# Two sets of four PSUM banks for W_down's seven Strassen products, and halo rows with high and low weight parts on their own column groups

## The chip, the cores and the metric

The kernel runs on one core of one Trainium2 chip. The metric is the device time of one execution in microseconds (us), as the median of several runs of the same program. A core has five engines with instruction queues of their own: PE (TensorE, matrix products into the eight banks of PSUM), DVE (VectorE), ACT (ScalarE), POOL (GpSimd) and SP (SyncE, which here issues the DMAs). They wait for each other through semaphores.

## The reference, cut to what matters

One decoder layer over 1024 tokens and 16 meta tokens, in float32:

```
h  = concat(meta, x)                                   # (1040, 1024)
xn = rms_norm(h, mix_pre_g)
mix = [ rms_norm(SSD(xn)), rms_norm(stick_breaking_attention(xn)) ] @ w_out
h  = h + rms_norm(mix, mix_post_g)
xn = rms_norm(h, ffn_pre_g)
gu = xn @ w_up                                         # (., 2 * 2816)
g  = causal_dwconv3(gu[:, :2816])                      # 3 taps, looks 2 tokens back
f  = (gelu(g) * gu[:, 2816:]) @ w_down                 # (., 1024)
h  = h + rms_norm(f, ffn_post_g)
return h[16:]
```

Because the convolution looks two tokens back, the last two meta tokens (the halo rows) go through the output projection and the first norms too.

## The kernel before, in words

**Arithmetic.** A float32 product is made of three products: each operand is split into a high part (a copy to the float32r type by ACT) and a low part (the operand less its high part), and high x high, low x high and high x low are summed in PSUM.

**Stages.** Norm and projections, SSD, attention (with W_out's first half as filler work on PE), W_out's second half with the norms behind it, W_up by a seven-product Strassen scheme, then W_down, from 1531 us to the end. In the attention stage (L971 on) only PE's order is written out by hand, and the other engines' order is made by the framework's planner. From the sixth row block of W_out's second half to the end (L1400 to L1788) the orders of PE, DVE, ACT and POOL are as the code writes them.

**W_down (L1549 to L1788).** The tokens are two halves of four row blocks t = 0 to 3, the 2816 rows of w_down 11 pairs p, the 1024 output columns two halves. `DOWN` (L38) lists seven products in the order 1, 2, 3, 6, 5, 7, 4; each is 11 steps, one for each pair, 77 steps s in all (`steps2`, L1551). `down_mm` (L1643) issues a step: for each of the four row blocks (order 3, 0, 1, 2) three matmuls of 128x512. Each product sums in four banks of its own. When a product is done, `evac2` (L1654) carries the banks into four groups of SBUF sums `facc[h, hf, t]` (h: half of the tokens, hf: half of the columns): by ACT copies for products 1 and 3, by DVE adds for the rest, two for each row block after products 5 and 7; after product 6 another four DVE adds join sums in SBUF (L1768). These jobs go to a list, `todo`, of which one is taken in each loop step.

The loop (L1718) does in step s: `down_mm(s)`; loads; `split_step(s + 3)` (L1568), in which ACT makes the high parts and DVE the low parts of the two operands of step s + 3, in a ring of three buffers, so that it waits for step s to end; for product 6 DVE first makes the operand t2 = b22 - b11 (L1579). Then come sums of w_down's blocks by `W_SUMS` (L1588: b11 in steps 15 + 2k, b21 in 16 + 2k and 41 + k, b12 in 37 + k, for k = 0 to 10), and one job of `todo`. In the last 14 steps (`LATE`, L1552) POOL instead of DVE makes the low part of the weight operand (L1582). The very last step has buffers of its own, and is split ahead of its turn (L1754 to L1758).

A finished row block gets its tail: `half_tail` (L1682: ACT sums the squares, DVE multiplies by the gain), `scale_tail`, `close_tail` (L1695: POOL adds the two halves and takes the power -0.5) and `end_tail` (L1700: DVE scales and adds the residual, SP stores). The tails of the first half of the tokens run from `todo` during product 7. The last four steps run row block by row block (L1722 to L1733), each block followed by `evac2` for product 4 and its tail.

**Halo rows.** `halo_rows` (L901) multiplies the two rows with W_out's halves: once in the attention stage (L1014), once before W_out's second half (L1067). Each of the four 32-column groups of PE holds a quarter of the output columns (256), and sums 8 blocks x (high, low). ACT copies the four quarters out of PSUM (L910) and SP stores them (L911) to `halod[half]`. `halo_block` (L1167) reads both, scales each by its own factor (L1173, L1175) and runs the norms of `after` (L1095).

Of the kernel before, what the change touches and what calls it, by code (L numbers as in the profile page):

```python
# [16 lines left out]
P = 128  # L17
# [34 lines left out]
def tile_layer(ctx: ExitStack, tc: tile.TileContext, x, meta, rows, parts,  # L52
# [16 lines left out]
    def psum_mm(name):  # L69
        return ps.tile([P, 512], F32, tag="mm", name=name, bufs=2)  # L70
# [62 lines left out]
    halod = [dr.tile([2, D], F32, name=f"halod{n}", tag=f"halod{n}") for n in range(2)]  # L133
# [767 lines left out]
    def halo_rows(pool, half, y0, w, acc):  # L901
        for k in range(8):
            for s in range(2):
                for c in range(4):
                    mm(acc[32 * c:32 * c + 2, 0:256], y0[:, k, :], w[k][s][:, 256 * c:256 * c + 256].bitcast(F32),
                       start=k == 0 and s == 0, stop=k == 7 and s == 1)
        mh = pool.tile([P, 256], F32, tag="ma", name=f"mh{half}", bufs=1)
        for c in range(4):
            rows_ = slice(32 * c, 32 * c + 2)
            nc.scalar.activation(mh[rows_], acc[rows_, 0:256], AF.Copy)  # L910
            nc.sync.dma_start(out=halod[half][:, 256 * c:256 * c + 256], in_=mh[rows_])  # L911
# [255 lines left out]
    def halo_block():  # L1167
        mt, mo = wp_f32("whi", "mb0")[:2], wp_f32("wlo", "mo0")[:2]
        for n, r in enumerate((r_ssd, r_sb)):
            dst = mt if n == 0 else mo  # L1170
            nc.sync.dma_start(out=dst, in_=halod[n])
            if n == 0:
                nc.vector.tensor_scalar(mt, mt, r[:2, 0:1], None, op0=ALU.mult)  # L1173
            else:
                nc.vector.scalar_tensor_tensor(mt, mo, r[:2, 0:1], mt, op0=ALU.mult, op1=ALU.add)  # L1175
# [376 lines left out]
    n2, LATE = len(steps2), 14  # L1552
# [15 lines left out]
    def split_step(s):  # L1568
        n, a, b, p = steps2[s]
        if s < n2 - 1:  # L1570
            hi = wp.tile([P, 2, 512], F32R, tag="whi", name=f"dh{s}", bufs=WB)
            lo = wp.tile([P, 2, 512], F32R, tag="wlo", name=f"dl{s}", bufs=WB)
            hi, lo = ([t[:, k] for k in range(2)] for t in (hi, lo))
        else:
            hi, lo = ([da.tile([P, 512], F32R, tag=f"b11{2 * k + e}", name=f"d{e}{k}{s}") for k in range(2)] for e in range(2))
        sub = nc.vector.tensor_tensor
        if n == 6:
            wd["t2", p] = db.tile([P, 512], F32, tag="t2", name=f"t2_{p}", bufs=2)
            sub(wd["t2", p], wd["b22", p], wd["b11", p], op=ALU.subtract)  # L1579
        for k, raw in enumerate((araw.pop(s), wd[b, p])):  # L1580
            nc.scalar.activation(hi[k], raw, AF.Copy)  # L1581
            (nc.gpsimd.tensor_tensor if k and s >= n2 - LATE else sub)(lo[k], raw, hi[k].bitcast(F32), op=ALU.subtract)  # L1582
        dops[s] = hi, lo
# [59 lines left out]
    def down_mm(s, tbs):  # L1643
        n, a, b, p = steps2[s]
        hi, lo = dops[s]
        for t in tbs:
            if p == 0:
                banks[t] = psum_mm(f"dn{n}_{t}") if t == 3 else pse.tile([P, 512], F32, tag="dn", name=f"dn{n}_{t}",
                                                                        bufs=6)
            c = slice(t * P, (t + 1) * P)  # L1650
            for i, (u, v) in enumerate(((hi, hi), (lo, hi), (hi, lo))):
                mm(banks[t], u[0][:, c], v[1], start=(p == 0 and i == 0), stop=(p == NPR - 1 and i == 2))  # L1652

    def evac2(n, t, acc):  # L1654
        add = nc.vector.tensor_tensor
        if n == 1:
            nc.scalar.activation(facc[1, 0, t], acc, AF.Copy)
        elif n == 2:
            add(facc[0, 0, t], acc, facc[1, 0, t], op=ALU.add)
        elif n == 3:  # L1660
            nc.scalar.activation(facc[0, 1, t], acc, AF.Copy)
        elif n == 6 or n == 4:
            add(facc[1, 0, t], acc, facc[1, 0, t], op=ALU.add)
        elif n == 5:
            add(facc[0, 1, t], acc, facc[0, 1, t], op=ALU.add)
            add(facc[1, 1, t], acc, facc[1, 0, t], op=ALU.add)
        elif n == 7:
            add(facc[1, 0, t], acc, facc[1, 0, t], op=ALU.add)
            add(facc[1, 1, t], acc, facc[1, 1, t], op=ALU.add)
# [12 lines left out]
    def half_tail(h, t, hf):  # L1682
        fg, ht, ms = tails[h, t]
        f = facc[h, hf, t]
        c = slice(512 * hf, 512 * hf + 512)
        junk = db.tile([P, 512], F32, tag="t2", name=f"jt{h}{t}{hf}", bufs=2)
        nc.scalar.activation(junk, f, AF.Square, scale=D ** -0.5, accum_out=ms[:, hf:hf + 1])
        nc.vector.tensor_tensor(fg[:, c], f, gfp[:, c], op=ALU.mult)
# [22 lines left out]
    last_u = probs[-1]  # L1711
    todo = []
# [5 lines left out]
    for s in range(n2):  # L1718
        n, a, b, p = steps2[s]
        if s > 2 and s < n2 - 4:  # L1720
            down_mm(s, (3, 0, 1, 2))
        elif s == n2 - 4:  # L1722
            for act in todo:
                act()
            for t in range(4):
                for k in range(4):
                    down_mm(s + k, (t,))
                evac2(n, t, banks[t])
# [8 lines left out]
        elif s == 5:  # L1737
# [4 lines left out]
            for h in range(2):  # L1742
                for hf in range(2):
                    for t in range(4):
                        facc[h, hf, t] = db.tile([P, 512], F32, tag=f"fa{h}{hf}{t}", name=f"facc{h}{hf}{t}")
# [6 lines left out]
        if s + 5 < n2:  # L1752
# [10 lines left out]
        if p == NPR - 1:  # L1763
            for t in (3, 0, 1, 2):
                todo.append(lambda n=n, t=t, acc=banks[t]: evac2(n, t, acc))
            if n == 6:
                for t in range(4):
                    todo.append(lambda t=t: nc.vector.tensor_tensor(facc[0, 1, t], facc[0, 1, t], facc[1, 0, t],  # L1768
                                                                    op=ALU.add))
            elif n == 5:  # L1770
# [73 lines left out]
```

## Time and profile before

| | us |
|---|---|
| median of 3 runs | 1757.07 |
| lowest and highest | 1756.71, 1760.06 |
| the profiled execution | 1754.64 |
| its span | 1752.8 |
| PE busy in the span | 1711.4 |
| DVE, ACT, POOL busy | 1127.2, 820.2, 890.3 |
| W_down: first and last matmul begin | 1531.2, 1744.6 |

The profile is of one execution. Times in it count from the start of the span; an instruction's line is that of the kernel's text, and "out<-in" are the names of its tiles. In a row of the timeline the first number is the start, the second the duration (or, where x is over 1, the time from the first start to the last end), and the bracket says how long the engine sat idle before and what ended that. In a row of groups the numbers behind the bar are busy time in us, mean duration in ns and idle time before, with its releasers. In a row of stretches there follow, behind the stretch, its length, PE's busy time with the count of matmuls, the granted clock, the DMA share and GB/s; a matmul that overlaps an edge counts. Matmuls are pipelined, so each lasts longer (0.39 us) than the spacing of their starts. In a row of one tile or line, the numbers are the shortest, median and longest duration in ns, the first and last start, and the shapes. A row of waits gives us in total, times, and the longest. SPq rows are issues of DMAs, and in the rows of issues the last number is the time from issue to landing.

### The profile page before, as it was taken

The page shows a single profiled execution, that of the slowest core. Times are in us where ns is not written, and L with a number is a line of the kernel's source. Part 1 is how long each engine was busy: PE and PEld are TensorE (multiplying, and loading weights), DVE is VectorE, ACT ScalarE, POOL GpSimd, SP SyncE. Part 2 cuts the span into 40 slices and gives each one's busy share as a digit, 9 for nine tenths or more (in the row PEclk, how much of TensorE's full clock was granted, in tenths as well). Part 3 has the DMA queues.
Part 4 walks back from the last instruction along what each step waited for, and adds up shares of the span by engine and source line. Part 5 has one row for each costly group of instructions (what it writes and reads, how often), then busy time and mean ns, then how long its engine had stood idle before and what let it go on. Part 6 is the DMA issues. An engine that isn't in the chain of part 4 may idle for free. (4 is left out here: it accounts for less than half of the span.)

```text
span 1752.8 us, 28312 instructions
## 1 busy us (share of the span) xinstructions
PE 1711.4 (98%) x11358; PEld 1505.3 (86%) x11358; DVE 1127.2 (64%) x1225; ACT 820.2 (47%) x1363; POOL 890.3 (51%) x664
## 2 busy tenths in 40 slices
PE   7999999999999999999899989999999999999997
PEld 6999899788999998998678778889998888888885
DVE  5652964875676686668430457676666666757988
ACT  5423653554566566568453344533333333344453
POOL 4323663585566576556451233487776777400015
PEclk9999999999999999999999999999999999999999
DMA  4143343231011110112214543133332222395334
GB/s 161 50 116 93 107 128 105 65 103 38 26 37 37 38 35 27 37 60 74 81 49 145 199 156 132 62 119 98 106 106 91 90 91 90 122 331 185 96 121 162
DMA packets 90655, 173.87 MB, mean 99 GB/s; under 512 B 10694, under 2 KB 35798, under 8 KB 90524
## 3 DMA queue, kind: packets, MB, share of 16 engines
q1 hardware_dynamic: 90524, 172.07, 30.6%
q8 instruction: 89, 1.46, 0.3%
q14 instruction: 42, 0.34, 0.1%
HBM read 122.32 MB, written 49.72 MB: 98 GB/s over the span
## 5 line engine op out<-in xcount | busy, mean ns | idle before, releaser
L764 POOL TENSOR_TENSOR bt<-bt,kp 128x256 f32<-128x256 f32 (+7 forms) x128 | 212.7, 1681 | 180.4 <-DVE kp L762 150.7
L762 DVE TENSOR_TENSOR_SCAN kp<-kp,hold 128x272 f32<-128x272 f32 (+7 forms) x128 | 184.0, 1478 | 26.2 <-ACT kp L755 17.2
L1197 POOL TENSOR_TENSOR wlo<-wr,whi 128x1024 fp32r<-128x1024 f32 x43 | 107.5, 2508 | 38.0 <-ACT whi L1196 38.0
L1652 PE MATMUL dn<-dl,dh 128*128 128x512 f32 x304 | 118.7, 390 | 1.2 <-POOL dl L1582 1.2
L1652 PE MATMUL dn<-dh,dl 128*128 128x512 f32 x304 | 118.6, 390 | 0.1
L1652 PE MATMUL dn<-dh 128*128 128x512 f32 x304 | 118.5, 390 | 0.0
L1697 POOL TENSOR_TENSOR fms<-fms 128x1 f32<-128x1 f32 x8 | 5.6, 694 | 197.9 <-ACT dh L1581 185.8
L755 ACT ACTIVATE kp<-z 128x288 f32<-128x288 f32 (+6 forms) x112 | 82.6, 737 | 47.8 <-PE z L754 22.1
L1581 ACT ACTIVATE dh<-ar 128x512 fp32r<-128x512 f32 x76 | 48.1, 632 | 112.0 <-PE dn L1652 77.4
L1196 ACT ACTIVATE whi<-wr 128x1024 fp32r<-128x1024 f32 x43 | 45.6, 1060 | 114.8 <-PE fX L1254 68.3
L163 PE MATMUL pj_v<-xs,wh_v 128*128 128x400 f32 (+2 forms) x384 | 94.9, 334 | 0.0
L163 PE MATMUL pj_k<-xs,wh_k 128*128 128x400 f32 (+2 forms) x384 | 94.3, 332 | 0.0
L1326 DVE SCALAR_TENSOR_TENSOR ga<-gr,pp,ga 128x1024 f32<-128x1024 f32 x44 | 71.4, 1622 | 34.7 <-ACT ga L1319 33.9
L163 PE MATMUL pj_q<-xs,wh_q 128*128 128x386 f32 (+2 forms) x384 | 93.7, 331 | 0.0
L778 ACT ACTIVATE th<-tw 128x1024 f32<-128x1024 f32 (+2 forms) x96 | 75.7, 818 | 38.0 <-PE tw L776 37.8
L163 PE MATMUL pj_X<-xs,wh_X 128*128 128x400 f32 (+2 forms) x384 | 93.0, 329 | 0.0
L163 PE MATMUL pj_z<-xs,wh_z 128*128 128x386 f32 (+2 forms) x384 | 91.5, 326 | 0.0
L730 DVE CAST qh<-q 128x128 fp32r<-128x128 f32 x64 | 44.1, 690 | 63.9 <-PE z L754 63.6
L776 PE MATMUL tw<-ident,bt 128*128 128x128 f32 x576 | 78.1, 279 | 5.9 <-ACT bt L756 3.0
L1582 DVE TENSOR_TENSOR dl<-ar,dh 128x512 fp32r<-128x512 f32 x76 | 58.4, 768 | 39.1 <-ACT dh L1581 35.9
L756 ACT ACTIVATE bt<-z 128x288 f32<-128x288 f32 (+6 forms) x112 | 82.9, 740 | 0.0
L936 PE MATMUL mo<-woa,yh 128*128 128x512 f32 x256 | 82.4, 396 | 0.0
(556 smaller groups left out, 5532.3 us busy)
## 6 DMA issues: line engine op xcount, KB each, us to landing
wr<-in_w_up SPq DMA_DIRECT2D x44, 512.0 KB, 4.1
fds<-ga SPq DMA_DIRECT2D x44, 256.0 KB, 2.0
b<-in_w_down SPq DMA_DIRECT2D x44, 256.0 KB, 4.7
ar<-fds SPq DMA_DIRECT2D x44, 256.0 KB, 2.6
fda<-ga SPq DMA_DIRECT2D x33, 256.0 KB, 4.5
ar<-fda SPq DMA_DIRECT2D x33, 256.0 KB, 3.0
yk<-yd SPq DMA_DIRECT2D x16, 512.0 KB, 4.5
wor<-in_w_out SPq DMA_DIRECT2D x12, 512.0 KB, 3.9
```

The source lines that it names most:

```text
L163: mm(acc[:ncol, :n - s], a[:, k, :ncol], xs[c0][:, b, k, s:n], start=(k == 0 and j == 0), stop=(k == KB - 1 and j == 2))
L755: nc.scalar.activation(kp[:, :, a:a + w], z[:, :, :w], AF.Sigmoid, scale=-QSCALE)
L756: nc.scalar.activation(bt[:, :, a:a + w], z[:, :, :w], AF.Sigmoid, scale=QSCALE)
L762: nc.vector.tensor_tensor_scan(kp[:, j][:, ::-1], kp[:, j][:, ::-1], hold[:, L - n:L][:, ::-1], 0.0, op0=ALU.mult, op1=ALU.max)
L764: nc.gpsimd.tensor_tensor(bt[:, j, 0:m], bt[:, j, 0:m], kp[:, j, 1:m + 1], op=ALU.mult)
L776: nc.tensor.transpose(tw[:, j, b, :], bt[:, j, c0:c0 + P], ident)
L778: nc.scalar.activation(th[:, :, :nb, :], tw[:, :, :nb, :], AF.Copy)
L936: mm(acc, u[:, k, :], v[:, cs], start=(k == 0 and j == 0), stop=(k == 7 and j == 2))
L1197: nc.gpsimd.tensor_tensor(l, raw, h.bitcast(F32), op=ALU.subtract)
L1326: nc.vector.scalar_tensor_tensor(v, self.g[jj][:, :, i:i + 256], fconv_w[:, j, i:i + 1], v, op0=ALU.mult, op1=ALU.add)
L1582: (nc.gpsimd.tensor_tensor if k and s >= n2 - LATE else sub)(lo[k], raw, hi[k].bitcast(F32), op=ALU.subtract)
L1652: mm(banks[t], u[0][:, c], v[1], start=(p == 0 and i == 0), stop=(p == NPR - 1 and i == 2))
```

## The change

- W_down's products go in the order 1, 2, 6, 5, 3, 7, 4 and sum in two sets of banks, A and B (`BANK`). Only products 1, 2 and 5 clear their banks. Product 6 sums onto 1, 7 onto both, 4 onto all three (A); 3 sums onto 5 (B). Between them `evac2` copies or adds the running sum into `facc`: ACT copies after products 1, 6 and 5, one DVE add for each row block after 2, 3 and 7, nothing after 4, whose tail reads the bank itself. The joining adds go.
- After products 5 and 7 the evacuation stands in the loop, directly behind the step's matmuls, since the next product goes on in the same banks; after 1, 2, 6 and 3 it goes to `todo` as before.
- All low parts are DVE's. The last step uses the ring; three steps instead of four run row block by row block at the end.
- The sum for b11 moves from steps 15 + 2k to 18 + k.
- In `halo_rows` column groups 0 and 1 take the high part and 2 and 3 the low part, 512 columns each; the four results of two rows x 512 are copied and stored in two rounds of 256 columns through one buffer, into four tensors `halod`, which `halo_block` reads and sums one after the other.

```diff
-DOWN = [(1, "a11", "b11"), (2, "a12", "b21"), (3, "s4", "b22"), (6, "s2", "t2"), (5, "s1", "b11"), (7, "s3", "b12"),
+DOWN = [(1, "a11", "b11"), (2, "a12", "b21"), (6, "s2", "t2"), (5, "s1", "b11"), (3, "s4", "b22"), (7, "s3", "b12"),
         (4, "a22", "b21")]
+BANK = {1: "A", 2: "B", 6: "A", 5: "B", 3: "B", 7: "A", 4: "A"}
...
     def halo_rows(pool, half, y0, w, acc):
         for k in range(8):
-            for s in range(2):
-                for c in range(4):
-                    mm(acc[32 * c:32 * c + 2, 0:256], y0[:, k, :], w[k][s][:, 256 * c:256 * c + 256].bitcast(F32),
-                       start=k == 0 and s == 0, stop=k == 7 and s == 1)
-        mh = pool.tile([P, 256], F32, tag="ma", name=f"mh{half}", bufs=1)
-        for c in range(4):
-            rows_ = slice(32 * c, 32 * c + 2)
-            nc.scalar.activation(mh[rows_], acc[rows_, 0:256], AF.Copy)
-            nc.sync.dma_start(out=halod[half][:, 256 * c:256 * c + 256], in_=mh[rows_])
+            for c in range(4):
+                mm(acc[32 * c:32 * c + 2, :], y0[:, k, :], w[k][c // 2][:, 512 * (c % 2):512 * (c % 2) + 512].bitcast(F32),
+                   start=k == 0, stop=k == 7)
+        for a in (0, 256):
+            mh = pool.tile([P, 256], F32, tag="ma", name=f"mh{half}_{a}", bufs=1)
+            for c in range(4):
+                b = 512 * (c % 2) + a
+                rows_ = slice(32 * c, 32 * c + 2)
+                nc.scalar.activation(mh[rows_], acc[rows_, a:a + 256], AF.Copy)
+                nc.sync.dma_start(out=halod[2 * half + c // 2][:, b:b + 256], in_=mh[rows_])
...
-        for n, r in enumerate((r_ssd, r_sb)):
+        for n, r in enumerate((r_ssd, r_ssd, r_sb, r_sb)):
             dst = mt if n == 0 else mo
             nc.sync.dma_start(out=dst, in_=halod[n])
...
     def split_step(s):
         n, a, b, p = steps2[s]
-        if s < n2 - 1:
...
+        hi = wp.tile([P, 2, 512], F32R, tag="whi", name=f"dh{s}", bufs=WB)
+        lo = wp.tile([P, 2, 512], F32R, tag="wlo", name=f"dl{s}", bufs=WB)
...
         for k, raw in enumerate((araw.pop(s), wd[b, p])):
-            nc.scalar.activation(hi[k], raw, AF.Copy)
-            (nc.gpsimd.tensor_tensor if k and s >= n2 - LATE else sub)(lo[k], raw, hi[k].bitcast(F32), op=ALU.subtract)
+            nc.scalar.activation(hi[:, k], raw, AF.Copy)
+            sub(lo[:, k], raw, hi[:, k].bitcast(F32), op=ALU.subtract)
...
-        for at, args in ((15 + 2 * k, ("b11", "b12", "b11", ALU.subtract)), (16 + 2 * k, ("b21", "b21", "b22", ALU.subtract)),
+        for at, args in ((18 + k, ("b11", "b12", "b11", ALU.subtract)), (16 + 2 * k, ("b21", "b21", "b22", ALU.subtract)),
...
             for i, (u, v) in enumerate(((hi, hi), (lo, hi), (hi, lo))):
-                mm(banks[t], u[0][:, c], v[1], start=(p == 0 and i == 0), stop=(p == NPR - 1 and i == 2))
+                mm(banks[BANK[n], t], u[:, 0, c], v[:, 1, :], start=(n in (1, 2, 5) and p == 0 and i == 0),
+                   stop=(p == NPR - 1 and i == 2), skip_group_check=n not in (1, 2, 5))
...
+        dst = facc[{1: (0, 0), 2: (0, 0), 6: (0, 1), 5: (1, 1), 3: (0, 1), 7: (1, 1)}[n] + (t,)]
+        if n in (1, 6, 5):
+            nc.scalar.activation(dst, acc, AF.Copy)
+        else:
+            add(dst, acc, dst, op=ALU.add)
...
     def half_tail(h, t, hf):
-        f = facc[h, hf, t]
+        f = banks["A", t] if (h, hf) == (1, 0) else facc[h, hf, t]
...
-        if s > 2 and s < n2 - 4:
+        if s > 2 and s < n2 - 3:
             down_mm(s, (3, 0, 1, 2))
-        elif s == n2 - 4:
+            if p == NPR - 1 and n in (5, 7):
+                for t in (3, 0, 1, 2):
+                    evac2(n, t, banks[BANK[n], t])
+        elif s == n2 - 3:
             for act in todo:
                 act()
             for t in range(4):
-                for k in range(4):
+                for k in range(3):
                     down_mm(s + k, (t,))
-                evac2(n, t, banks[t])
                 half_tail(1, t, 0)
...
-        if s == n2 - 6:
-            fetch_a(n2 - 1)
-        split_step(s + 3)
-        if s == n2 - 5:
-            split_step(n2 - 1)
+        if s + 3 < n2:
+            split_step(s + 3)
...
         if p == NPR - 1:
-            for t in (3, 0, 1, 2):
-                todo.append(lambda n=n, t=t, acc=banks[t]: evac2(n, t, acc))
-            if n == 6:
-                for t in range(4):
-                    todo.append(lambda t=t: nc.vector.tensor_tensor(facc[0, 1, t], facc[0, 1, t], facc[1, 0, t],
-                                                                    op=ALU.add))
-            elif n == 5:
+            if n in (1, 2, 6, 3):
+                for t in (3, 0, 1, 2):
+                    todo.append(lambda n=n, t=t, acc=banks[BANK[n], t]: evac2(n, t, acc))
+            if n == 3:
                 for t in range(4):
                     def whole(t=t):
                         open_tail(0, t)
```

More of the change, by code (lines that the diff above doesn't have):

```diff
@@ L132, in tile_layer @@
     mixd = [dr.tile([P, D], F32, name=f"mixd{t}", tag=f"mixd{t}") for t in range(NT)]
-    halod = [dr.tile([2, D], F32, name=f"halod{n}", tag=f"halod{n}") for n in range(2)]
+    halod = [dr.tile([2, D], F32, name=f"halod{n}", tag=f"halod{n}") for n in range(4)]
     zd = [dr.tile([4, P, L], F32, name=f"zd{g}", tag=f"zd{g}") for g in range(2)]
@@ L1646, in down_mm @@
         for t in tbs:
-            if p == 0:
-                banks[t] = psum_mm(f"dn{n}_{t}") if t == 3 else pse.tile([P, 512], F32, tag="dn", name=f"dn{n}_{t}",
-                                                                        bufs=6)
+            if (BANK[n], t) not in banks:
+                nm = f"dn{BANK[n]}{t}"
+                banks[BANK[n], t] = psum_mm(nm) if t == 3 else pse.tile([P, 512], F32, tag=nm, name=nm)
             c = slice(t * P, (t + 1) * P)
             for i, (u, v) in enumerate(((hi, hi), (lo, hi), (hi, lo))):
-                mm(banks[t], u[0][:, c], v[1], start=(p == 0 and i == 0), stop=(p == NPR - 1 and i == 2))
+                mm(banks[BANK[n], t], u[:, 0, c], v[:, 1, :], start=(n in (1, 2, 5) and p == 0 and i == 0),
+                   stop=(p == NPR - 1 and i == 2), skip_group_check=n not in (1, 2, 5))
     def evac2(n, t, acc):
         add = nc.vector.tensor_tensor
[L1656 to L1663, printed above, removed]
-        elif n == 5:
[L1665 to L1669, printed above, removed]
+        dst = facc[{1: (0, 0), 2: (0, 0), 6: (0, 1), 5: (1, 1), 3: (0, 1), 7: (1, 1)}[n] + (t,)]
[3 more added lines that the diff above has]
+            add(dst, acc, dst, op=ALU.add)
     slots = [ta.tile([P, 4 * HW], F32, tag=f"{n}{e}", name=f"slot{n}{e}") for n in ("b22", "t4") for e in "hl"]
@@ L1711, in tile_layer @@
     last_u = probs[-1]
+    n2 = len(steps2)
     todo = []
@@ L1741, in tile_layer @@
             db = down.enter_context(tc.tile_pool(name="db", bufs=1, side="left"))
-            for h in range(2):
-                for hf in range(2):
-                    for t in range(4):
-                        facc[h, hf, t] = db.tile([P, 512], F32, tag=f"fa{h}{hf}{t}", name=f"facc{h}{hf}{t}")
+            for h, hf in ((0, 0), (0, 1), (1, 1)):
+                for t in range(4):
+                    facc[h, hf, t] = db.tile([P, 512], F32, tag=f"fa{h}{hf}{t}", name=f"facc{h}{hf}{t}")
             gfp = db.tile([P, D], F32, name="gfp", tag="gfp")
```

10 lines of the change are left out of this document (1 added, 9 removed).

## The prediction

> **What bounds the kernel now.** I read the page's busy line first, then TensorE (PE) in two stretches of W_down, then the engines beside it there, the tail, and the halo rows.
>
> ```profile
> PE 1711.4 (98%) x11358; PEld 1505.3 (86%) x11358; DVE 1127.2 (64%) x1225; ACT 820.2 (47%) x1363; POOL 890.3 (51%) x664
> ...
> 1699.80:1713.40 13.60, 13.60 (x61) 1.00 0.61 228
> 1713.40:1725.90 12.50, 11.93 (x49) 1.00 0.66 231
> ```
>
> PE is the bound: an edit pays only by PE's own work, by a gap in PE, or behind the last matmul. The change leaves PE's work alone: W_down keeps 77 steps (7 products of 11 row pairs) of 12 matmuls. The two stretches of W_down's matmuls give the pace: 60 spacings in 13.60 us, 0.227 us each, so 2.72 us a step. The next 48 spacings (steps 67 to 70) should take 10.88 and take 12.50. So PE has gaps, and the question is which the change closes and which it opens.
>
> **Removed: the low parts on GpSimd (POOL), steps 63 to 76.** The gaps in steps 67 to 70 are 12.50 - 10.88 = 1.6 us. At the end, where steps 73 to 76 run side by side, one row block (t) after the other:
>
> ```profile
> 1732.53 0.39 PE L1652 MATMUL dn<-dl,dh 128*128 128x512 f32 x1
> ...
> 1734.52 0.51 PE L1652 MATMUL dn<-dl,dh 128*128 128x512 f32 x1 [0.64 <-POOL dl L1582]
> ...
> 1736.55 0.39 PE L1652 MATMUL dn<-dh 128*128 128x512 f32 x1
> L1582 POOL TENSOR_TENSOR dl<-b,dh 128x512 fp32r<-128x512 f32 x13 | 21.2, 1647 | 4.7 <-ACT dh L1581 3.3 <-PE dn L1652 1.4
> L1582 DVE TENSOR_TENSOR dl<-ar,dh 128x512 fp32r<-128x512 f32 x74 | 57.0, 771 | 39.0 <-ACT dh L1581 35.9 <-DMA ar<-fda 3.1
> ```
>
> From 1732.53 to 1736.55 there are seven spacings: 4.02 us for 1.59, a gap of 2.43, ended by POOL's low part. A POOL low part takes 1.65 us on average. In steady state a split by VectorE (DVE) alone looks like this (step 41 begins on PE, the split for step 43 starts):
>
> ```profile
> 1642.72 0.39 PE L1652 MATMUL dn<-dh 128*128 128x512 f32 x1
> 1642.73 0.68 DVE L1579 TENSOR_TENSOR t<-b,b 128x512 f32<-128x512 f32 x1
> ...
> 1642.97 0.63 ACT L1581 ACTIVATE dh<-ar 128x512 fp32r<-128x512 f32 x1 [1.57 <-issue]
> ...
> 1643.51 0.62 ACT L1581 ACTIVATE dh<-t 128x512 fp32r<-128x512 f32 x1
> ...
> 1643.64 0.69 DVE L1582 TENSOR_TENSOR dl<-ar,dh 128x512 fp32r<-128x512 f32 x1 [0.22 <-ACT dh L1581]
> ...
> 1644.25 0.68 DVE L1582 TENSOR_TENSOR dl<-t,dh 128x512 fp32r<-128x512 f32 x1
> ...
> 1644.85 0.68 DVE L1586 TENSOR_TENSOR b<-b,b 128x512 f32<-128x512 f32 x1
> ...
> 1648.16 0.39 PE L1652 MATMUL dn<-dh 128*128 128x512 f32 x1
> ```
>
> Step 40's buffers come free as step 41 begins; ScalarE (ACT) starts 0.25 us later, DVE's first low part at 0.92, the second at 1.53, done at 2.21. It is needed by the third matmul of step 43: 1648.16 + 0.45 = 5.89 after 1642.72. **The lead is about 3.7 us.** So steps 67 to 70 lose their gap: **-1.6**. At the end the last split waits for step 73's buffers and PE has steps 74 and 75 of the first row block between, six matmuls (1.36 us). The second low part is done at 2.21 and wanted two matmuls after 1.36, at 1.81: a gap of 0.4, 0.5 with the slower matmul after a gap. 2.43 becomes 0.5: **-1.9**. The dropped buffers for step 76 cost nothing else.
>
> **Moved: the sums of W_down's blocks, and product 6 ahead of 3.** Product 6 builds t2 in its split. Its splits now fall in loop steps 19 to 29, among the sums of b11 (one a step, 18 to 28), of b21 (every second step) and product 2's four evacuations (22 to 25). DVE instructions for steps 19 to 29: 4, 5, 4, 6, 5, 6, 5, 5, 4, 5, 3, in all 52. DVE issues one per 0.60 us (1643.64, 1644.25, 1644.85), so 2.72 us hold 4.5; before, no step there had over four. Five have been tried, in steps 44 to 47:
>
> ```profile
> 1655.08 0.69 DVE L1582 TENSOR_TENSOR dl<-b,dh 128x512 fp32r<-128x512 f32 x1
> 1655.68 1.29 DVE L1586 TENSOR_TENSOR b<-b,b 128x512 f32<-128x512 f32 x2
> 1656.88 0.69 DVE L1663 TENSOR_TENSOR facc<-dn,facc 128x512 f32<-128x512 f32 x1
> 1657.48 0.68 DVE L1582 TENSOR_TENSOR dl<-ar,dh 128x512 fp32r<-128x512 f32 x1
> ```
>
> There DVE no longer waits for ACT, and slips 0.29 us a step. In the new stretch a second delay joins: once DVE is late, ACT copies t2 only after DVE made it, so t2 to its low part takes 0.68 + 0.10 + 0.62 + 0.04 = 1.44 where two issue slots are 1.20: 0.24 a step (0.10 from DVE to ACT and 0.04 back are the lags of the tail's rows below and of 1643.51). Step 18 has four from 0.9 on, so DVE takes up step 19 at 0.9 + 4 x 0.60 - 2.72 = 0.6 after PE's mark. After the 49 instructions of ten steps it stands at 0.6 + 49 x 0.604 + 10 x 0.24 - 10 x 2.72 = 5.4; step 29's low part of t2 is then done at 5.4 + 1.44 + 0.73 (duration and lag) = 7.6, wanted at 5.9: 1.7 late. Where t2 follows directly the b11 sum that it reads, about 0.12 more each (a dependent pair starts 0.72 apart in the tail's rows, 1745.03 and 1745.75), three times in the late stretch: **+2.1**. Bounds: 0 (PE untouched, as in steps 44 to 47) and +5.7 (49 slots of the full 0.685 for 0.604: 4.0 on top of the 1.7).
>
> **Added: two evacuations in the loop, before PE may go on in the same banks.** After product 5 ACT copies; it is idle half the time, and PE returns to a bank after nine matmuls (2.04 us): 0. After product 7 (step 65) DVE adds, and stands behind the tail of row block 2:
>
> ```profile
> 1697.12 0.39 PE L1652 MATMUL dn<-dh 128*128 128x512 f32 x1
> 1698.81 0.55 POOL L1698 TENSOR_TENSOR fms<-fms,nhalf 128x1 f32<-128x1 f32 x1
> 1740.83 1.28 DVE L1706 SCALAR_TENSOR_TENSOR slotb22h<-slotb22h,fms 128x1024 f32<-128x1024 f32 x1
> ```
>
> Row block 0's tail shows the shape: the power is done at 1699.36, 2.24 after step 61 began. In the changed kernel DVE's 1.28 us then run from 2.28 to 3.56, that is 0.84 into step 66, and the first add ends at 0.84 + 0.69 = 1.53. PE wants that bank at 0: **+1.6** with the lag (the other three banks follow 0.68 apart, as PE does). Behind the adds wait splits with over 3 us of lead. Bounds 0 (tail early) and 2.2 (POOL's add stretched to its 1.08 of below).
>
> **Shortened: the tail.** The last rows:
>
> ```profile
> 1744.14 0.85 PE L1652 MATMUL dn<-d,d 128*128 128x512 f32 x3
> 1745.03 0.69 DVE L1663 TENSOR_TENSOR facc<-dn,facc 128x512 f32<-128x512 f32 x1 [0.16 <-PE dn L1652]
> 1745.75 0.69 DVE L1688 TENSOR_TENSOR slott4l<-facc,gfp 128x512 f32<-128x512 f32 x1
> 1745.81 0.63 ACT L1687 ACTIVATE jt<-facc 128x512 f32<-128x512 f32 x1 [2.04 <-DVE facc L1663]
> ...
> 1746.36 1.28 DVE L1706 SCALAR_TENSOR_TENSOR slott4h<-slott4h,fms 128x1024 f32<-128x1024 f32 x1
> 1746.61 1.08 POOL L1697 TENSOR_TENSOR fms<-fms 128x1 f32<-128x1 f32 x1 [1.06 <-ACT jt L1687]
> ...
> 1747.77 0.55 POOL L1698 TENSOR_TENSOR fms<-fms,nhalf 128x1 f32<-128x1 f32 x1
> 1748.35 1.41 DVE L1706 SCALAR_TENSOR_TENSOR slott4l<-slott4l,fms 128x512 f32<-128x512 f32 x2 [0.71 <-POOL fms L1698]
> ```
>
> The add of 1745.03 goes (0.69 and its lag, 0.75 in all); ACT squares out of the bank. But POOL's add ended with DVE's 1.28 us, and a row block now gets 9 matmuls (2.04 us) for DVE's 0.69 + 1.28. I take **-0.4**, between -0.75 (POOL free) and +0.3 (DVE late by some 0.3 a block).
>
> The Trainium skill's page "SBUF — State Buffer" (SBUF: two separate sides) says that GpSimd and a VectorE instruction with two SBUF inputs exclude each other for a whole instruction. The trace agrees: POOL's add took 1.08 us and ended 0.05 after DVE's. By it alone POOL's power would hold up DVE's 1.28 us, and the tail would give -0.4; without it -0.7.
>
> **Halo rows.**
>
> ```profile
> L905 PE MATMUL halo<-woa,y x128: 377/379/379, 856.3 to 863.0; 128*2 128x256 f32 x128
> 863.49 1.58 ACT L910 ACTIVATE mh<-halo 2x256 f32<-2x256 f32 x4 [5.41 <-PE halo L905]
> 865.09 0.61 ACT L755 ACTIVATE kp<-z 128x528 f32<-128x528 f32 x1
> 866.30 0.63 PE L776 MATMUL tw<-ident,bt 128*128 128x128 f32 x4 [0.78 <-issue]
> xsd<-xtk SPq DMA_DIRECT2D x8, 8.0 KB, 1.3
> 974.78 0.28 SPq L1171 DMA_DIRECT2D mb<-halod x1
> 989.93 1.26 DVE L1175 SCALAR_TENSOR_TENSOR mb<-mo,r_sb,mb 2x1024 f32<-2x1024 f32 x1
> 1014.73 1.04 ACT L1097 ACTIVATE mo<-mb 2x1024 f32<-2x1024 f32 x1
> PE x2tp L1116 <- DVE oxn L1110: 4.8, 1, 4.8
> ```
>
> 128 passes of 0.379 us in 6.7 us means that four column groups run at once: 32 rounds of 0.21 us. Each group streams 16 x 256 columns before and 8 x 512 after: the same. **0** (-0.1 at best).
>
> The skill's page "TensorEngine Tiling (Array Packing)" (Instruction Overhead) gives each matmul about 60 cycles of overhead, 25 ns at the 2.4 GHz of its page "TensorE: Matmul & The Clock Gate" (Part 1). An estimate from it is 0.8 us off the two halos for 32 rounds fewer in all, and -1.0 for the sum; the rounds here are already as long as their columns, so I keep 0.
>
> ACT gets four more copies (1.58 us) per halo, which wait for the first four's DMAs (1.3 us for a small one) in the same buffer. If they stand ahead of kp, PE's transposes at 866.30 come up to 3.2 us later; if the planner lets kp pass, 0. I take 0: it lets ready work pass elsewhere (974.78 is issued before the second halo's stores, 982). The halo block reads four parts for two: two loads and two 1.26 us steps, some 5.3 us. Its data stand ready at 991.19 and its norm starts at 1014.73, 23.5 us on: 0.
>
> **Sum:** -1.6 - 1.9 + 2.1 + 1.6 - 0.4 + 0 = -0.2. The profiled execution (1754.64; span 1752.8 and 1.84 around it) becomes 1754.4. The median of the runs shown is 2.43 higher, so I forecast **1756.9**.
>
> **The rivals.** A measurement can tell about 0.2%, 3.5 us, from no change. *No new bound* (0.24): DVE's slips stay inside the lead, as in steps 44 to 47, and the adds come in time: -1.6 - 1.9 - 0.4 = -3.9, 1753.2. Against it speaks the count of 52. *The halo chain moves a PE wait* (0.18, slower): PE already waits 4.8 us for a row block's norm (L1110), in a stretch where the halo rows' norm shares ACT, DVE and POOL. If that norm is placed by its data, what stands behind it comes 5.3 us later: 1762.2. It decides once the added loads use up the 23.5 us, or the planner moves the norm; the slack speaks against. *DVE far behind* (0.06): the +5.7 bound, 1760.5, up to 1763.7 with ACT's 3.2. *Column groups of high and low parts do not overlap* (0.02): two halos of 6.9 us double, 1770.7. The forecast holds 0.50. Faster by over 0.2%: 0.24; within: 0.50; slower: 0.26. The range 1752.0 to 1763.0 takes in the first two rivals; its ends leave out 0.08 or so each, by the spread around these sums.
>
> **What would show it.** Right: no PE wait for POOL in W_down; a PE gap near product 6's end, ended by DVE's low part; one of 1.6 us at step 66, ended by an L1663-like add; the last matmul to the end 0.4 shorter; halo rows still 6.8 us. Wrong: PE at 2.72 a step through product 6, or gaps between 860 and 1060 that were not there.

## The result, and the profile after

The changed kernel takes 1759.01 us (median of 12 runs) where the kernel before takes 1758.22 (12 runs): a ratio of 1.0003, with a 95% interval of 0.9996 to 1.0011. No difference can be told, as forecast.

The profiled execution of the changed kernel has a span of 1757.7 us, that of the kernel before 1752.8. Most of these 4.9 us are not the change's. Up to the first halo rows PE, DVE, ACT and POOL run the same instructions in the same order in both kernels, and yet the first W_out matmul begins at 841.67 before and at 844.89 after. Two stretches hold these 3.2 us. Here they are in the kernel before and then in the changed one (stretch, length, busy time with instruction counts of the five engines, granted TensorE clock, DMA share, GB/s):

```profile
320.00:360.00 40.00, 36.64 (x233) 30.35 (x232) 33.56 (x41) 25.58 (x64) 30.37 (x26) 1.00 0.24 67
400.00:440.00 40.00, 39.96 (x297) 35.85 (x295) 24.07 (x38) 21.43 (x37) 24.88 (x34) 1.00 0.14 41
```

```profile
320.00:360.00 40.00, 36.63 (x225) 30.31 (x224) 32.04 (x41) 25.86 (x64) 28.87 (x25) 0.96 0.24 67
400.00:440.00 40.00, 39.96 (x295) 35.31 (x294) 19.92 (x36) 20.00 (x36) 24.46 (x33) 0.96 0.15 41
```

In each, the granted clock is 0.04 lower, which is 1.6 us of 40. So spans of two single executions are not compared below; stages and waits are.

**W_down after.** The same kind of view: first to last matmul, steps 28 to 31, steps 65 and 66, and steps 67 to 70. At 2.72 us a step, four steps take 10.88, two 5.44.

```profile
1536.26:1749.78 213.52, 211.64 (x925) 172.48 (x923) 156.42 (x252) 101.00 (x190) 8.18 (x14) 1.00 0.55 179
...
1612.43:1624.62 12.19, 12.14 (x49) 8.39 (x47) 11.70 (x20) 4.25 (x9) 0.00 (x0) 1.00 0.30 86
...
1714.79:1722.26 7.47, 5.72 (x25) 4.42 (x24) 7.03 (x13) 3.53 (x8) 1.43 (x2) 1.00 0.88 291
1722.26:1733.14 10.88, 10.88 (x49) 9.01 (x48) 9.41 (x19) 6.45 (x14) 1.66 (x2) 1.00 0.62 210
```

In the kernel before, the whole stretch was 213.40 (1531.19 to 1744.60). Steps 67 to 70 now run without a gap. Steps 28 to 31 lose 1.3 us (step 32 another 0.4, so 1.7 in all), steps 65 and 66 lose 2.0. Gains and losses meet.

Note that PE's busy time hides the gap of steps 28 to 31 (12.14 of 12.19): matmuls that start late one by one are drawn longer. The starts show it, in the timeline of PE and of DVE beside it:

```profile
1612.05 0.69 DVE L1579 TENSOR_TENSOR dl<-t,dh 128x512 fp32r<-128x512 f32 x1
1612.66 0.68 DVE L1583 TENSOR_TENSOR b<-b,b 128x512 f32<-128x512 f32 x1
1613.26 0.68 DVE L1658 TENSOR_TENSOR facc<-dnB,facc 128x512 f32<-128x512 f32 x1
1613.86 0.68 DVE L1576 TENSOR_TENSOR t<-b,b 128x512 f32<-128x512 f32 x1
1614.46 0.68 DVE L1579 TENSOR_TENSOR dl<-ar,dh 128x512 fp32r<-128x512 f32 x1
1615.24 0.69 DVE L1579 TENSOR_TENSOR dl<-t,dh 128x512 fp32r<-128x512 f32 x1
...
1615.60 0.40 PE L1649 MATMUL dnA<-dh,dl 128*128 128x512 f32 x1
1615.99 0.50 PE L1649 MATMUL dnA<-dl,dh 128*128 128x512 f32 x1
```

DVE idles for 0.10 us only here, in front of the last low part. That low part, of t2 for step 29, ends at 1615.93, and PE's matmul behind it starts at 1615.99. From one t2 low part to the next are 3.19 us for five instructions (five slots of 0.60, and 0.18 more in front of the last), against the step's 2.72.

**Step 66**, DVE, POOL and PE:

```profile
1716.27 0.69 DVE L1579 TENSOR_TENSOR dl<-b,dh 128x512 fp32r<-128x512 f32 x1
1716.48 0.88 POOL L1687 TENSOR_TENSOR fms<-fms,nhalf 128x1 f32<-128x1 f32 x1
1717.39 1.28 DVE L1695 SCALAR_TENSOR_TENSOR slott4h<-slott4h,fms 128x1024 f32<-128x1024 f32 x1 [0.44 <-POOL fms L1687]
1718.59 2.48 DVE L1658 TENSOR_TENSOR facc<-dnA,facc 128x512 f32<-128x512 f32 x4
1719.42 0.47 PE L1649 MATMUL dnA<-dh 128*128 128x512 f32 x1 [1.75 <-DVE facc L1658]
```

DVE sits idle for 0.44 us, waiting for POOL's power, then scales row block 2, and only then adds the banks that PE wants.

**The halo block.** DVE's order before and then after, at row block 1's norm:

```profile
999.24 1.29 DVE L1100 SCALAR_TENSOR_TENSOR mb<-mb,rs_mo,gpost 128x1024 f32<-128x1024 f32 x1 [3.85 <-POOL rs_mo L190]
1000.57 1.23 DVE L1101 TENSOR_TENSOR mb<-mb,xr 128x1024 f32<-128x1024 f32 x1
```

```profile
1002.97 1.28 DVE L1102 SCALAR_TENSOR_TENSOR mb<-mb,rs_mo,gpost 128x1024 f32<-128x1024 f32 x1 [3.85 <-POOL rs_mo L191]
1004.17 1.26 DVE L1177 SCALAR_TENSOR_TENSOR mb<-mo,r_sb,mb 2x1024 f32<-2x1024 f32 x1
1005.37 1.21 DVE L1103 TENSOR_TENSOR mb<-mb,xr 128x1024 f32<-128x1024 f32 x1
```

One of the two added steps stands between the row block's gain and its residual add, which come 2.40 us apart instead of 1.33. The waits of PE in this stage, after:

```profile
PE x2tp L1118 <- DVE oxn L1112: 6.3, 1, 6.3
```

It was 4.8. This wait existed, and it grew by 1.4 us; how much of that reaches the end of the stage is told with halo_only below. The halo matmuls themselves take 7.05 us in each half (860.58 to 867.63 and 978.39 to 985.44) where they took 7.09.

**The tail**, from the last matmul on, its end being 1750.17:

```profile
1749.78 0.39 PE L1649 MATMUL dnA<-dl,dh 128*128 128x512 f32 x1
1750.26 0.60 ACT L1676 ACTIVATE jt<-dnA 128x512 f32<-128x512 f32 x1 [1.35 <-PE dnA L1649]
...
1750.98 0.69 DVE L1677 TENSOR_TENSOR slott4l<-dnA,gfp 128x512 f32<-128x512 f32 x1 [0.16 <-ACT jt L1676]
1751.03 0.19 POOL L1686 TENSOR_TENSOR fms<-fms 128x1 f32<-128x1 f32 x1 [1.22 <-ACT jt L1676]
1751.30 0.55 POOL L1687 TENSOR_TENSOR fms<-fms,nhalf 128x1 f32<-128x1 f32 x1
1751.59 1.28 DVE L1695 SCALAR_TENSOR_TENSOR slott4h<-slott4h,fms 128x1024 f32<-128x1024 f32 x1
1752.79 1.41 DVE L1695 SCALAR_TENSOR_TENSOR slott4l<-slott4l,fms 128x512 f32<-128x512 f32 x2
```

ACT squares 0.73 us earlier after the last matmul than before, and the last scaling ends at 4.03 after it instead of 4.77. But the end of the span is 7.55 behind the last matmul instead of 7.81: only 0.26 are left. The transfers of the stores end 6.38 us behind the last matmul where they ended 6.50. And the tail differs between executions: the changed one takes 7.55 us in five of the traces below, 7.67 and 7.96 in two, and the old one 7.70 to 7.82 in three. So the gain is some 0.1 to 0.3 us.

### The profile page after: what moved, and what is told of

The parts are those of the page before. It is cut to its first block, busy times and chain, and to the rows that moved or that the text cites. A ratio compares the mean times of both kernels' runs of the same rounds, so it can differ in the third digit from the quotient of the medians.

```text
span 1757.7 us, 28050 instructions
## 1 busy us (share of the span) xinstructions
PE 1712.8 (97%) x11230; PEld 1502.4 (85%) x11230; DVE 1116.7 (64%) x1221; ACT 825.2 (47%) x1375; POOL 869.4 (49%) x650
## 5 line engine op out<-in xcount | busy, mean ns | idle before, releaser
L1579 DVE TENSOR_TENSOR dl<-ar,dh 128x512 fp32r<-128x512 f32 x77 | 53.2, 691 | 50.9 <-ACT dh L1578 50.8
L792 PE MATMUL av<-th,v 128*64 128x128 f32 x1152 | 77.5, 279 | 0.0
L777 PEld LDWEIGHTS tw<-ident,bt 128*128 128x128 f32 x576 | 65.7, 142 | 13.6 <-ACT bt L757 5.2
L928 POOL TENSOR_TENSOR yl<-yk,yh 128x1024 fp32r<-128x1024 f32 x16 | 40.3, 2520 | 71.7 <-ACT yh L927 63.2
```

The lines of the kernel that those rows point to most:

```text
L777: nc.tensor.transpose(tw[:, j, b, :], bt[:, j, c0:c0 + P], ident)
L792: mm(av[halves[j], :], v[:, kb, halves[j]], th[:, j, b, :], start=kb == 0, stop=kb == i)
```

## Experiments

Theory: the change wins 1.6 us in steps 67 to 70, 1.9 at W_down's end and some 0.3 in the tail, and gives back 1.7 near product 6's end (DVE's count of instructions), 2.0 at step 66 (the evacuation behind a scaling), and 1.4 at PE's wait for the norm (the halo block's extra steps). The rivals stand with each run. Times are ratios to the kernel before on the same chip; "W_down" is from the start of its first to that of its last matmul, "wait" PE's wait before x2tp, "tail" from the last matmul's end to the span's end, each from the trace.

| kernel | ratio (95% interval) | W_down | wait | tail |
|---|---|---|---|---|
| before | 1 | 213.40 | 4.85 | 7.81 |
| changed | 1.0003 (0.9996 to 1.0011) | 213.52 | 6.25 | 7.55 |
| wdown_only | 1.0003 (0.9994 to 1.0012) | 213.54 | 4.75 | 7.67 |
| halo_only | 1.0005 (0.9996 to 1.0014) | 213.33 | 6.30 | 7.70 |
| spread | 0.9988 (0.9979 to 0.9997) | 210.07 | 6.21 | 7.55 |
| own_buffers | 1.0014 (1.0005 to 1.0023) | 213.50 | 7.10 | 7.55 |
| best | 0.9981 (0.9972 to 0.9989) | 210.08 | 4.94 | 7.96 |
| low_dve | 0.9981 (0.9973 to 0.9990) | 210.39 | 4.86 | 7.82 |
| b21_later | one run | 211.78 | 6.30 | 7.55 |
| evac_first | one run | 211.74 | 6.37 | 7.55 |
| tail_swap | one run | 210.06 | 4.89 | 7.16 |

**wdown_only** takes the halo edits (`halod`, `halo_rows`, `halo_block`) out of the changed kernel:

```diff
-    halod = [dr.tile([2, D], F32, name=f"halod{n}", tag=f"halod{n}") for n in range(4)]
+    halod = [dr.tile([2, D], F32, name=f"halod{n}", tag=f"halod{n}") for n in range(2)]
...
-        for n, r in enumerate((r_ssd, r_ssd, r_sb, r_sb)):
+        for n, r in enumerate((r_ssd, r_sb)):
```

> The changed W_down with the halo rows of the kernel before. Account theory (the changed kernel loses 1.7 us near product 6's end, 2.0 at step 66 and 1.4 in TensorE's wait before the x2tp transposes near 1027 us, and wins 1.6 in steps 67 to 70, 1.9 at the end and 0.3 in the tail): that wait is 4.8 to 4.9 us again instead of 6.25, the two gaps in W_down stay at 1.7 and 2.0, and the time is 0.1 us below the kernel before (ratio 0.9999), 1.4 below the changed one. Rival (the longer wait was a difference between two executions, not the halo rows): the wait can be anything from 4.8 to 6.3, and the time is that of the changed kernel.

**halo_only** puts the same edits alone into the kernel before.

> The changed halo rows with the W_down of the kernel before. Account theory: the two extra VectorE steps of the halo block stand in VectorE's order ahead of a row block's residual add (L1101 before) and of the next bank read, the wait before x2tp is 6.2 to 6.3 us, W_down has the gaps of the kernel before (3.9 us in all), and the time is 1.4 us above the kernel before (ratio 1.0008). Rival (a difference between executions): the wait is 4.8 to 4.9 and the ratio 1.0000. The two sets of halo matmuls last 7.0 to 7.1 us each by either.

PE's waits in that stage, wdown_only and then halo_only:

```profile
PE x2tp L1117 <- DVE oxn L1111: 4.8, 1, 4.8
```

```profile
PE x2tp L1117 <- DVE oxn L1111: 6.3, 1, 6.3
```

The wait follows the halo edits: it is 4.75 to 4.94 in the five traces with the old halo rows and 6.21 to 6.37 in the five with the new ones as the change has them. The rival, a difference between executions, falls. The times of the two runs cannot tell 1.4 us: the intervals reach from 1 us below to 2.5 us above the kernel before.

In W_down nothing changes by these edits: wdown_only keeps the gaps of the changed kernel (213.54 us in all), halo_only those of the kernel before (213.33).

But not all of the longer wait reaches the end of the stage. Behind this wait PE's granted clock is below 1 in every trace. Here are the same 46 spacings of PE's matmuls, counted from the wait's end, in best (old halo rows) and then in spread (new ones), both of which come below:

```profile
1031.84:1042.58 10.74, 10.74 (x47) 8.86 (x47) 6.74 (x8) 5.42 (x9) 2.38 (x5) 0.78 0.56 166
```

```profile
1031.08:1041.39 10.31, 10.31 (x47) 8.58 (x48) 6.41 (x7) 4.62 (x8) 2.17 (x4) 0.82 0.66 223
```

The wait of spread is 1.28 us longer, and 0.43 of it come back here, since more of the time at the lower clock passes while PE waits (in both traces the clock is at one half for 6.8 us, from 44 us after the second halo matmuls on). From the end of the second halo matmuls to W_down's first matmul the five traces with the new halo rows, as the change has them, take 550.8 to 551.3 us, and those with the old ones 550.2 to 550.4, except for the kernel before with 549.5 (its clock in this stretch was 0.85, that of the other four 0.78). So an estimate from the medians of these spans, 551.2 and 550.3, is that the halo edits cost 0.9 us, not 1.4.

**spread** relieves DVE at both places in W_down of the changed kernel:

```diff
-        for at, args in ((18 + k, ("b11", "b12", "b11", ALU.subtract)), (16 + 2 * k, ("b21", "b21", "b22", ALU.subtract)),
+        for at, args in ((18 + k, ("b11", "b12", "b11", ALU.subtract)), (31 + k, ("b21", "b21", "b22", ALU.subtract)),
...
-        if todo:
+        if todo and s != 64:
             todo.pop(0)()
```

> The changed kernel with two edits in VectorE's order: the first b21 sums at steps 31 to 41 instead of every second step from 16 to 36, and no job taken from the list at step 64, so that the scaling of row block 2's tail (1.28 us) comes behind the evacuation after product 7. Account theory (VectorE's count of instructions makes the gap near product 6's end, the 1.28 us that of step 66): TensorE runs at 2.72 us a step through steps 22 to 32, the gap at step 66 is at most 0.2 us, and the time is 3.5 us below the changed kernel, 2.3 below the kernel before (ratio 0.9987). Rival (another limit: ScalarE's copy of t2, the loads of b12 and b22): the gap near product 6's end stays 1.7 us and only 1.9 go. Rival (the sums' load is only moved): a new gap of 1 to 2 us in steps 33 to 45.

Its stretches: the whole of W_down, and one around product 6's end.

```profile
1535.08:1745.15 210.07, 209.96 (x925) 173.19 (x923) 156.29 (x252) 101.29 (x190) 7.91 (x14) 1.00 0.55 181
1609.00:1627.00 18.00, 18.00 (x81) 14.93 (x80) 15.69 (x26) 7.85 (x14) 0.00 (x0) 1.00 0.37 102
```

No gap is left but 0.3 us at step 66 and 0.5 at the end, and none comes up where the sums went. The 3.4 us are there in the trace, and the ratio is 0.9988 where 0.9987 was expected.

**b21_later** and **evac_first** make one of these two edits each (the first line and the second).

> The changed kernel with the first b21 sums at steps 31 to 41 alone. Account theory: no gap near product 6's end (steps 28 to 32 at 2.72 us), the gap at step 66 stays 2.0 us. Rival (the two gaps share a cause): both shrink.

> The changed kernel with no job at step 64 alone, so that the scaling of 1.28 us comes behind the evacuation after product 7. Account theory: the gap at step 66 is at most 0.2 us, the 1.7 us in steps 28 to 32 stay. Rival (the evacuation itself, 4 adds of 0.69 us and ScalarE's and VectorE's lags, costs it): a gap of 0.7 us or more stays at step 66.

W_down's whole stretch, b21_later and then evac_first:

```profile
1535.40:1747.18 211.78, 209.94 (x925) 173.09 (x923) 156.67 (x252) 101.28 (x190) 8.18 (x14) 1.00 0.55 180
```

```profile
1536.51:1748.26 211.75, 211.62 (x925) 172.57 (x923) 156.21 (x252) 101.02 (x190) 7.91 (x14) 1.00 0.55 180
```

Each takes away its own gap and leaves the other: 1.74 and 1.77 us of 213.52, and 3.45 together. At step 66 0.27 us stay in evac_first, a little more than expected, since the adds still come behind a split. The two gaps have separate causes, as the theory has it.

**best** is spread with the halo rows of the kernel before.

> The two edits of VectorE's order of the run before (first b21 sums at steps 31 to 41, no job at step 64) on the changed W_down, with the halo rows of the kernel before. Account theory (the terms add up): no gap above 0.2 us in W_down, the wait before x2tp 4.7 to 4.9 us, the time 3.7 us below the kernel before (-1.6 - 1.9 - 0.3 and 0.1 for what is left at step 66), ratio 0.9979, and 1.4 below the run with these two edits alone. Rival (what the halo rows cost is taken up elsewhere, as the times of the two single parts leave open): ratio 0.9985 to 0.9990, as with the two edits alone.

The wait is 4.94 and W_down 210.08. 0.3 us of gap are left at step 66 and 0.5 at the end, as in spread, where at most 0.2 was expected. The ratio 0.9981 lies at the theory's 0.9979, but its interval reaches up to 0.9989 and does not shut out the rival's 0.9985 to 0.9990. What the halo edits cost is shown by the wait and the span of the stage, not by the time.

**low_dve** is the kernel before with one constant changed:

```diff
-    n2, LATE = len(steps2), 14
+    n2, LATE = len(steps2), 0
```

> The kernel before with one edit: the low parts of its last 14 steps by VectorE (LATE = 0). Theory 1 (all that the change wins in W_down comes from this part; the two sets of banks win nothing by themselves): steps 67 to 70 at 10.9 us, the gap at the end 0.5, ratio 0.9980 (-3.5 us). Theory 2 (VectorE cannot take them beside the eight adds after product 7 and the tails, and the bank sets are what makes room): gaps of 1 us or more come back in steps 66 to 76, ended by VectorE, and the ratio is 0.9990 or more.

W_down's whole stretch, and steps 67 to 70:

```profile
1535.69:1746.09 210.40, 210.21 (x925) 173.21 (x923) 168.11 (x271) 98.67 (x186) 8.87 (x13) 1.00 0.56 183
1717.94:1728.82 10.88, 10.88 (x49) 9.01 (x48) 10.19 (x18) 4.61 (x8) 1.43 (x2) 1.00 0.81 266
```

Theory 1 holds, and it says more than any other run: the one constant wins 3.0 us in W_down and gives 0.9981, as much as best. DVE has 271 instructions in this stretch, 19 more than in the changed kernel (252), and PE does not wait for them. At the end 1.0 us of gap is left, not 0.5: four low parts in a row (1735.13 to 1737.63) feed the last two steps there. **So the two sets of banks save DVE 19 instructions that nobody was waiting for.** The order that they bring (product 6 early, among b21's sums, and evacuations inside the loop) opened the two gaps that used up what the low parts had won. With those closed, W_down is 0.3 us shorter than with the constant alone.

**own_buffers** keeps the changed kernel's halo rows, but reads each part into a buffer of its own, so that the last two loads need not wait for the step before them:

```diff
+        parts = [mt, mo, wp_f32("wlo", "mo1")[:2], wp_f32("whi", "mo2")[:2]]
...
-            dst = mt if n == 0 else mo
+            dst = parts[n]
...
-                nc.vector.scalar_tensor_tensor(mt, mo, r[:2, 0:1], mt, op0=ALU.mult, op1=ALU.add)
+                nc.vector.scalar_tensor_tensor(mt, dst, r[:2, 0:1], mt, op0=ALU.mult, op1=ALU.add)
```

> The changed kernel, with a buffer of its own for each of the four parts that the halo block reads, so that the last two loads go out together; VectorE's instructions are the same, but both extra steps then stand ahead of the row block's gain step (L1102) instead of between it and its residual add. Account theory (their place in VectorE's order costs 1.4 us): the wait before x2tp is 4.8 to 5.0 us and the time 1.4 below the changed kernel (equal to the kernel before within 0.2). Rival (their number or the extra transfers cost it, wherever they stand): the wait stays 6.2 to 6.3 us.

Neither was right: the wait is 7.10, and the kernel is slower than the one before (1.0014, 1.0005 to 1.0023). Its timeline of DVE and POOL there, and then POOL's in the changed kernel:

```profile
996.39 4.60 DVE L1178 SCALAR_TENSOR_TENSOR mb<-mo,r_sb,mb 2x1024 f32<-2x1024 f32 x2
996.92 3.00 POOL L928 TENSOR_TENSOR yl<-yk,yh 128x1024 fp32r<-128x1024 f32 x1 [9.11 <-ACT yh L927]
1000.00 1.07 POOL L190 TENSOR_SCALAR ms_mo<-oss 128x1 f32<-128x1 f32 x1
1001.16 0.58 POOL L191 TENSOR_TENSOR rs_mo<-ms_mo,nhalf 128x1 f32<-128x1 f32 x1
1001.77 1.28 DVE L1102 SCALAR_TENSOR_TENSOR mb<-mb,rs_mo,gpost 128x1024 f32<-128x1024 f32 x1 [0.78 <-POOL rs_mo L191]
```

```profile
999.57 2.40 POOL L928 TENSOR_TENSOR yl<-yk,yh 128x1024 fp32r<-128x1024 f32 x1 [9.11 <-ACT yh L927]
1002.06 0.22 POOL L190 TENSOR_SCALAR ms_mo<-oss 128x1 f32<-128x1 f32 x1
```

The steps now stand where DVE had been idle, ahead of the row block's gain. But POOL was at work there, on the chain that DVE was idle for. The second step took 3.30 us (997.69 to 1000.99) instead of 1.26, POOL's subtraction (the low part of y) 3.00 instead of 2.40, and its next instruction 1.07 instead of 0.22. From DVE's last bank read (995.72) to the gain (1001.77) are 6.05 us, where the changed kernel has 4.59 (998.38 to 1002.97). The residual add then follows the gain after 1.32 us again. The rest of the longer wait is ACT's wait for the next load of y (4.25 us here, 3.78 in the changed kernel, 3.44 in the one before); why the load comes later is not shown. That the two engines shut each other out is read from these rows; no run takes it alone.

The same pair stands on the way to PE's wait itself, in the kernel before too. In the changed kernel, DVE and POOL:

```profile
1027.47 3.87 DVE L1112 SCALAR_TENSOR_TENSOR mo<-mb,rs_ff,gffn 2x1024 f32<-2x1024 f32 x1 [1.14 <-POOL rs_ff L191]
1031.27 1.27 DVE L1112 SCALAR_TENSOR_TENSOR oxn<-mb,rs_ff,gffn 128x1024 f32<-128x1024 f32 x1
1027.93 2.33 POOL L928 TENSOR_TENSOR yl<-yk,yh 128x1024 fp32r<-128x1024 f32 x1
```

The first row is the halo rows' own last step. It takes 3.87 us in all eleven traces, and DVE's same operation on the same shape took 1.27 at 1021.96. Behind it stands the row block's oxn that PE waits for, whose factor POOL had ready at 1027.96. What the other order of these two would win, no run shows.

**tail_swap** turns round, in best, the two reads of the bank in the last four tails:

```diff
+        first = h == 1 and hf == 0
+        if first:
+            nc.vector.tensor_tensor(fg[:, c], f, gfp[:, c], op=ALU.mult)
         nc.scalar.activation(junk, f, AF.Square, scale=D ** -0.5, accum_out=ms[:, hf:hf + 1])
-        nc.vector.tensor_tensor(fg[:, c], f, gfp[:, c], op=ALU.mult)
+        if not first:
+            nc.vector.tensor_tensor(fg[:, c], f, gfp[:, c], op=ALU.mult)
```

> The run with both order edits and the old halo rows, with one more edit in the tails that read a bank: VectorE's multiply by the gain stands ahead of ScalarE's square instead of behind it. Theory (the two reads of one bank go one after the other in the order of the code, and it is VectorE's order that ends the kernel): in the last row block VectorE's multiply starts within 0.1 us of the last matmul's end instead of 0.8 after it, ScalarE's square 0.7 later than before, and the last two scalings start 0.0 to 0.3 us earlier (at 2.3 to 2.6 us after the last matmul's end instead of 2.6). Rival (the two engines read the bank side by side, and the multiply waited for something else): both start within 0.15 us of the last matmul's end, and the last scalings start 0.6 us earlier.

The tail, behind a last matmul that ends at 1746.96:

```profile
1746.99 0.69 DVE L1676 TENSOR_TENSOR slott4l<-dnA,gfp 128x512 f32<-128x512 f32 x1 [0.16 <-PE dnA L1648]
1747.60 1.28 DVE L1698 SCALAR_TENSOR_TENSOR slott4h<-slott4h,fms 128x1024 f32<-128x1024 f32 x1
1748.06 0.60 ACT L1678 ACTIVATE jt<-dnA 128x512 f32<-128x512 f32 x1 [1.63 <-DVE slott4l L1676]
...
1749.68 1.41 DVE L1698 SCALAR_TENSOR_TENSOR slott4l<-slott4l,fms 128x512 f32<-128x512 f32 x2 [0.80 <-POOL fms L1690]
```

The reads go one after the other, in the order of the code: the rival falls. ACT's square starts 1.0 us later than in the changed kernel, where 0.7 was expected. The last scalings start 2.73 us after the last matmul's end, not at 2.3 to 2.6; here the theory missed (the changed kernel has 2.62, and best, which this run edits, 2.90). And yet the tail is the shortest of all, 7.16. What is earlier is the scaling of the row block before (0.64 instead of 1.42 in the changed kernel) and with it that block's store, issued 1.94 us after the last matmul's end instead of 2.72. It is a single run.

## Why the prediction was right

The time came out as forecast (1759.01 for 1756.9; 1.2 of the 2.1 us between them are the kernel before's own median, 1757.07 of three runs and 1758.22 of twelve). The mechanism held too: two gains from the low parts and two losses to DVE's load and order that meet them. That the sum came so near is partly luck: the two losses missed by 0.4 us each, in opposite directions, and a missing term of 0.9 us is less than the times can tell. Term by term:

- **Low parts off POOL, steps 67 to 70: -1.6.** Right. They take 10.88 us after, and with the constant alone too.
- **The end: 2.43 becomes 0.5.** Right. In the changed kernel the spacings of the late first block (from 1742.71) exceed 0.227 by 0.5 us in sum.
- **Product 6: +2.1.** Right in mechanism and place, 1.7 in size. DVE falls behind, the low part of t2 ends PE's wait, and putting b21's sums elsewhere (b21_later) takes the gap away and nothing else. The estimate took 0.24 us a step for t2's way through ACT and back; the rows show 0.18.
- **Step 66: +1.6.** Right in mechanism, 2.0 in size. The term was built on a power that ends 2.24 us into step 65. It ended 2.57 in (1717.36 after 1714.79), because POOL's power took 0.88 us, not 0.55, beside DVE's low part.
- **Evacuation after product 5: 0.** Right: no gap there.
- **Tail: -0.4.** It came out at -0.1 to -0.3, and for another reason than given. POOL's add was not held up (0.19 us). ACT reads the bank first, DVE's multiply waits for that (1750.98), and the scaling of the block before comes behind the multiply, so that block's store is issued 2.72 us after the last matmul's end, where it was 2.68. The scaling is done 0.74 earlier, but the end is the landing of stores, whose transfers end only 0.12 earlier. tail_swap, which issues that one store earlier, moves the end.
- **Halo rows on PE: 0; ACT's four more copies: 0.** Right. kp passed the second four copies after the first halo, and PE's transposes behind it have the same gap of 0.78 (to 870.50). The Trainium skill's page "TensorEngine Tiling (Array Packing)" (Instruction Overhead) gave an estimate of 0.8 us off for the rounds saved. The trace has 0.04 us for each of the two halos (7.09 to 7.05; the prediction's 6.7 to 6.9 us do not count the last round in full).
- **Halo block: 0. This step failed**: "Its data stand ready at 991.19 and its norm starts at 1014.73, 23.5 us on: 0." The slack is the halo block's own, and it was there. But its steps are on DVE, whose order is fixed when the program is made, and one of them stands ahead of a row block's residual add on the way to the norm that PE waits for: +1.4 in the wait, some +0.9 in the stage. The forecast had this as a rival, "the halo chain moves a PE wait", with +5.3; the place was right, but only one of the two steps got there, with 1.07 us, and ACT's longer wait for the next load of y (3.44 to 3.78) brought the other 0.34. So one of the prediction's signs of being wrong, a gap between 860 and 1060 that was not there, came up as a longer wait.

With the measured sizes the sum is -1.6 - 1.9 + 1.7 + 2.0 - 0.3 + 0.9 = +0.8 us; the ratio says +0.5 (-0.7 to +1.9). "No new bound" fell by its condition: DVE's slips did not stay inside the lead. What the prediction didn't ask is which edit the gains hang on. Both come with the low parts, and the bank sets were not needed for either.

## What to carry to other kernels

Count an engine's instructions per step wherever sums are moved. When a change is worth nothing, look for the single edit that wins and for the one that pays it back: here one constant gave the whole gain. Ask of an added step not whether its own chain has slack, but whose instruction stands behind it on its engine, and what a neighbour is doing in SBUF while the engine is idle there.

## What the runs showed of the hardware

- An idle DVE is not free for an SBUF step while POOL works in SBUF: a step of 1.26 us took 3.30 beside POOL's subtraction, and stretched that from 2.40 to 3.00 and the next POOL instruction from 0.22 to 1.07. Two partitions are enough for it (all these DVE steps are 2x1024). The Trainium skill's page "SBUF — State Buffer" (SBUF: two separate sides) has GpSimd and a VectorE instruction with two SBUF inputs exclude each other for whole instructions, and these rows agree. In the prediction the same rule was applied to the tail, where POOL's add took 0.19 us: there DVE was reading a bank of PSUM. POOL's power in the changed kernel's tail (1751.30 to 1751.85) did not hold up DVE's scaling either, which began at 1751.59 and took the 1.28 us that it takes elsewhere; by the prediction's reading of the rule it would have.
- In this kernel ACT and DVE read one PSUM bank one after the other, whichever the code puts first: the second starts 0.7 us later, released by the first. Whether the chip or the framework asks for this, no run here shows.
- Two executions of the same instructions differ by 3.2 us before the first changed one, in stretches where the granted clock is 0.96. A change of 1 to 2 us in this kernel is seen in gaps and waits, which repeat to 0.1 or 0.2 us, and hardly in times. A longer wait is not a stage as much longer: behind PE's wait the clock averaged 0.78 to 0.85 over the next 10 us, and by 46 matmuls later 1.28 us more of waiting (spread against best) had become 0.85.
